# A second split buffer for projected q and k columns, and a planner that keeps TensorE on products of one width

## The chip, the cores and the metric

One NeuronCore of a Trainium2 chip runs the whole program. The metric is the device time of one execution in microseconds, as the median of the runs shown. TensorE (PE) multiplies, VectorE (DVE), ScalarE (ACT) and GpSimd (POOL) do the elementwise work, and SyncE (SP) issues nearly all DMAs.

## The reference, cut to what matters

One step of a two-layer decoder trunk in float32, for a prompt of 2048 tokens of width 1024 and for 8 sample sequences of one new token each with 2048 cached ones. Every layer is one input projection, two mixers that run as parallel branches, one output projection and a LayerNorm.

```python
def even_mixer(x, past_kv, w_in, w_sp, b_sp):          # layer 0
    h = jnp.einsum('btd,de->bte', x, w_in)
    u, v, gate_a, q, k, vb, gate_b = _split(h, EVEN_SPLITS)   # 7 x 512 columns
    ...
    out_a = chunk_spatial_gate(u, v, w_sp, b_sp) * jax.nn.silu(gate_a)
    o = stick_breaking(q, k, v, q_pos, k_pos)          # 8 heads of 64
    out_b = o * jax.nn.silu(gate_b)

def stick_breaking(q, k, v, q_pos, k_pos):
    z = jnp.einsum('bqhd,bkhd->bhqk', q, k) * HEAD_DIM ** -0.5
    log_keep = jnp.where(mask, jax.nn.log_sigmoid(-z), 0.0)
    later = lax.cumsum(log_keep, axis=3, reverse=True) - log_keep
    att = jnp.where(mask, jnp.exp(jax.nn.log_sigmoid(z) + later), 0.0)
    return jnp.einsum('bhqk,bkhd->bqhd', att, v)
```

Layer 1 (`odd_mixer`) selects the 256 best keys of each query by an indexer (four small heads), does softmax attention over them with a relative bias (8 query heads, 2 key heads), and beside it pools causally over windows of 2 to 16 tokens.

## The kernel before, in words

The prompt is cut into four blocks of 512 tokens (i = 0 to 3). Layer 0 of a block is its first phase `p0(i)` (load x and transpose it, 28 projections of 128 columns each), then attention `mixer_b(i)`, then the output projection `out_proj`. Layer 1 is `p1a` and `p1b` (projections), `c_tiles` (index, selection and attention for each 128 queries) and another `out_proj`. The phases of different blocks run beside each other, so that TensorE gets projections while attention waits for other engines.

Products of float32 accuracy on the projections are made of three in float32r: a number is split into a high part, rounded to float32r, and the rest. `split` does it: ScalarE casts (line 637), VectorE or GpSimd subtracts (line 643). A projection (`proj`) is 8 x 3 products of 128x512 into a bank `pp` of PSUM (lines 724, 725, 726); the weights are loaded as `wr` and split into `wh` and `wl` (lines 648, 650, 653). Of the 28 projections of `p0` the first four are q and the next four are k. Each is split into a tile `q_hl` or `k_hl` of 128 x 2 x 512, and two DMAs store it to `qsc` or `ksc` in DRAM, from where attention loads it in another layout. All of these tiles share one tag, `hl`, with one buffer: the cast of the next must wait until both stores of the last have landed. For k a plain copy `kT` (line 872) is made as well, transposed on TensorE (`ps_k`, line 882) and written out.

In `mixer_b` a product `z` (line 1014) gives scores, ScalarE makes `P` of it (lines 1018, 1021), VectorE scans it (line 1028), TensorE transposes it (`ps_p`, line 1051) and multiplies by v (`av`, line 1060). In layer 1 the same steps are `z_c` (line 1756), `zt` with the maximum `mx` (line 1758) and the exponent (line 1774), the transposes `ps_pc` (line 1787) and `av_c` (line 1801). The index has `z_i` (line 1446). `av`, `av_c`, `ps_rb` (line 1821) and the sample group's `ps_sav` (line 1984) use half or a quarter of TensorE's columns, two or four such products side by side; the code calls their kind "h" and a group of them that write one bank is placed as one. All other products use the full array.

What sets the order on each engine is a planner, `Order`, that runs when the program is built. It knows all instructions, what each needs, and which buffers it takes; `cost` gives each a busy time and a latency in ns. `plan` places them in a list for each engine: among those that are ready, the one with the lowest rank, which is the latest start that `latest` allowed it in an earlier plan, in ns. `settle` makes 15 pairs of plans and keeps one; `keep` fixes that order as dependencies. So a changed cost or rule may move any instruction of the program, on each engine, but adds or removes none. A change from or to kind "h" is priced with `TILED`, 150 ns.

Of the kernel before, what the change touches and what calls it, by code (L numbers as in the profile page):

```python
# [22 lines left out]
P = 128  # L23
# [62 lines left out]
class Order:  # L86
# [1 line left out]

    ENGINES = {"PE": "PE", "DVE": "DVE", "Activation": "ACT", "Pool": "POOL", "SP": "SP"}
    SEM, DMA_START, DMA_END, RATE = 200, 700, 1500, 280.0  # L90
    TILED = 150
    GUESSES = ((1.0, 200), (1.0, 250), (1.04, 230))
    ROUNDS, DRAWS, SPREAD = 5, 2, 0.05
    TAIL = {"ACT": 100, "POOL": 45, "DVE": 75}
# [136 lines left out]
    def cost(self, n):  # L231

        i, e = self.ins[n], "PE" if self.halves(n) else self.eng[n]
        aps = self.aps(i)
        if e is None or not aps:
            return (400, 400) if type(i).__name__ == "BassTileConditionalBlock" else (30 if e else 0, 30)
        if i.opcode == "TensorLoad":
            return 1300, 1300
        k = max(self.size(x) for x in aps)
        ps = any(self.space(x) == PSUM for x in aps)  # L240
        full = [x for x in i.ins if getattr(x, "bass_ap", None) is not None and self.size(x) > 1]
        if "DMA" in i.opcode:
            out = [x for x in i.outs if getattr(x, "bass_ap", None) is not None][0]
            size = math.prod(n for _, n in out.ap) * (2 if out.dtype == BF16 else 4)
            runs = []
            for x in aps:
                r = 1
                for s, n in reversed(list(x.ap)):
                    if s != r:
                        break  # L250
                    r *= n
                runs.append(r)
            return 65 if e == "SP" else 900, size / (self.RATE * (1.2 if min(runs) >= 512 else 0.93))
        if e == "PE":
            k = self.size(i.outs[0])
            if i.is_transpose:
                return 109, 270
            if i.ins[0].dtype == F32R:
                return max(59, 3 + 0.4455 * k), 0.444 * k + 170
            if self.halves(n):  # L260
                return max(109, 1.8 * k * tuple(i.tile_size)[1] / P), max(222, 1.7 * k) + 170
            return max(223, 6 + 1.67 * k), max(222, 1.75 * k) + 170
        name = re.sub(r"_\d+$", "", i.outs[0].bass_ap.tensor.name)
        c = BUSY.get(f"{e} {name} {i.opcode} {k}")
        if c is not None:
            return c, c + self.TAIL[e]
        if e == "ACT":
            c = 70 + (0.82 if ps else 0.87) * k if i.opcode == "TensorCopy" else 70 + 0.83 * k if ps else 200 + 0.93 * k
            return c, c + 100
        if e == "POOL":  # L270
            c = {"TensorTensor": 15 + 2.4 * k, "Iota": 50 + 0.9 * k, "Memset": 40}.get(i.opcode, 180 + 0.78 * k)
            return c, c + 45
        ptr = sum(getattr(x, "bass_ap", None) is not None and self.size(x) == 1 for x in i.ins) if k > 1 else 0
        if getattr(i, "is_tensor_tensor_scan", False):
            c = 40 + 2.23 * k
        elif i.opcode == "TensorScalarPtr" and not ps and len(full) == 1 and len(i.outs) == 1:
            c = 65 + 0.54 * k + 60 * ptr
        elif i.opcode == "TensorScalarPtr" and len(i.outs) > 1:
            c = 150 + 1.05 * k
        else:  # L280
            c = 65 + 1.04 * k + 60 * ptr
        return c, c + 75
# [157 lines left out]
    def plan(self, rank):  # L440
# [41 lines left out]
        while count < N:  # L482
            while back and back[0][0] <= now:
                _, g, x = pop(back)
                free[g] += 1
                gone[g].append(x)
                take(g, now)
            while due and due[0][0] <= now:
                n = pop(due)[1]
                if eng[n] is not None:  # L490
                    push(ready[eng[n]], (rank[n], n))
                    continue
                count += 1
                for m in succ[n]:
                    release(m, now)
            moved, late = False, []
            for e, q in ready.items():
                while q and idle[e] <= now:
                    n, until = q[0][1], hold.get(self.OTHER.get(e), 0.0)
                    if ports[n] and until > now:  # L500
                        free_ = [x for x in q if not ports[x[1]] and now + cost[x[1]][0] <= until + self.SLACK]
                        if not free_:
                            late.append(until)
                            break
                        n = min(free_)
                        q.remove(n)
                        heapq.heapify(q)
                        n = n[1]
                    else:
                        pop(q)  # L510
                    s, (busy, lat) = now, cost[n]
                    if ports[n]:
                        hold[e] = s + max(40, busy - self.RELEASE[e])
                    if e == "PE" and now > idle[e] + 1 and kinds[n] == kind:
                        busy, lat = busy + self.RESTART, lat + self.RESTART
                    if e == "PE" and kinds[n] != kind:
                        s += self.TILED if "h" in (kinds[n], kind) else 0
                        kind = kinds[n]
                    self.begun[n] = s
                    if self.dma[n]:  # L520
                        dma_end = max(s + self.DMA_START, dma_end) + lat
                        done[n] = dma_end + self.DMA_END
                    else:
                        done[n] = s + lat
                    idle[e] = s + busy
                    self.order[e] += [*self.before.get(n, ()), *self.group.get(n, (n,))]
                    count += 1
                    moved = True
                    for m in succ[n]:
                        release(m, s + 1 if e == "PE" and eng[m] == "PE" else done[n] + self.SEM)  # L530
                    for t in tiles[n]:
                        g, u = home[t], self.uses[t]
                        if n == u[0]:
                            open_[g] = True
                            for m in u[1:]:
                                release(m, s)
                            take(g, s)
                        users[t] -= 1
                        if not users[t]:
                            push(back, (max(done[m] for m in u) + self.SEM, g, t))  # L540
            if not moved:
                then = [q[0][0] for q in (due, back) if q] + [idle[e] for e in ready if ready[e]]
                then = [x for x in then if x > now] + late
                assert then or count == N
                now = max([now] + [min(then)] if then else [now])
# [68 lines left out]
class Body:  # L614
# [230 lines left out]
    def p0(self, i, smp=None):  # L845
# [14 lines left out]

        for m in range(4):
            ps = yield from pj(12 + m)
            hl = self.loc.tile([P, 2, TB], F32R, tag="hl", name="q_hl", bufs=self.bufs["hl"])
            self.split(hl[:, 0], hl[:, 1], ps, "act", "dve")
            for a in range(2):
                nc.sync.dma_start(self.qsc[i][2 * m + a].rearrange("c p n -> p c n"),
                                  hl[64 * a:64 * a + 64].bitcast(F32))

        for m in range(4):
            ps = yield from pj(16 + m)  # L870
            kT = self.tok("kT")
            nc.scalar.copy(kT, ps)
            hl = self.loc.tile([P, 2, TB], F32R, tag="hl", name="k_hl", bufs=self.bufs["hl"])
            self.split(hl[:, 0], hl[:, 1], ps, "act", "dve")
            for a in range(2):
                nc.sync.dma_start(self.ksc[i][2 * m + a].rearrange("(c p) n -> p c n", c=2),
                                  hl[64 * a:64 * a + 64].bitcast(F32))

            def k_tail(m=m, kT=kT):
                pt = self.ps("ps_k", [P, NT, P])  # L880
                for t in range(NT):
                    nc.tensor.transpose(pt[:, t, :], kT[:, t * P:(t + 1) * P], self.idf)
                kt = self.tmp("k_tok").rearrange("p (t c) -> p t c", t=NT)
                nc.scalar.copy(kt, pt)
                nc.sync.dma_start(kv[rows, 0, m * P:(m + 1) * P].rearrange("(t p) c -> p t c", p=P), kt)

            tails.append(k_tail)
# [1583 lines left out]
```

## Time and profile before

| | |
|---|---|
| median of 3 runs | 2861.96 us (2861.57 to 2862.91) |
| the profiled execution's own time | 2859.05 us |
| its span, first to last instruction | 2857.3 us |
| mean granted TensorE clock | 0.975 |
| busy: PE, DVE, ACT, POOL | 95%, 72%, 56%, 27% |
| DMA | 523.50 MB, mean 183 GB/s |

Rows of a timeline read: start in us, duration in us, engine, line, operation, what it writes and reads, shapes, how many in a row were merged, and in brackets how long the engine had been idle and what ended that. A duration of a product on PE runs into the next one's, since products overlap: the time that a product holds the engine is read from start to start. Rows of waits read: engine and line, what it waited for, us in total, times, longest.

### The profile page before, as it was taken

To read this page: it belongs to the slowest core of one execution; us is meant where nothing else is said; L and a number is where in the kernel's file an instruction comes from. 1 tells how busy PE (TensorE), PEld (TensorE's weight loads), DVE (VectorE), ACT (ScalarE), POOL (GpSimd) and SP (SyncE) were. 2 spreads that over 40 slices of the span, in tenths; PEclk is the share of its full clock that TensorE was granted. 3 is DMA by queue.
4 is the path that set the end of the run, shared out by engine and by line. 5 is a ranking of instruction groups with operands and counts; after the bars stand their busy time and mean duration, and the time that the engine had idled before them with its cause. 6 is when DMAs were issued, how large, how long until landed. Compare 5 with 4: busy or idle time off the path is not lost. (4 is left out here: it accounts for less than half of the span.)

```text
span 2857.3 us, 52362 instructions
## 1 busy us (share of the span) xinstructions
PE 2708.1 (95%) x17490; PEld 2160.9 (76%) x17490; DVE 2058.0 (72%) x5557; ACT 1608.3 (56%) x3216; POOL 764.7 (27%) x1040
## 2 busy tenths in 40 slices
PE   7999999999999999998899999999989999999996
PEld 6886777867777687777567777777857889798985
DVE  3375467685766776646877888897898677888865
ACT  2433333344443435434566777786686677788863
POOL 0001103120110412123332432334321353435222
PEclk9999999999999999998999999999989999999998
DMA  7565867597677659545575456433656566667462
GB/s 216 165 181 172 257 198 227 175 292 212 186 211 206 217 176 299 164 148 157 148 198 160 142 166 165 125 100 100 192 181 162 173 210 182 209 202 254 134 196 70
DMA packets 536591, 523.50 MB, mean 183 GB/s; under 512 B 43183, under 2 KB 408904, under 8 KB 536287
## 3 DMA queue, kind: packets, MB, share of 16 engines
q1 hardware_dynamic: 526439, 484.29, 56.5%
q0 software_dynamic: 9856, 35.66, 3.9%
q8 instruction: 139, 2.28, 0.3%
q14 instruction: 157, 1.29, 0.1%
HBM read 430.27 MB, written 89.73 MB: 182 GB/s over the span
## 5 line engine op out<-in xcount | busy, mean ns | idle before, releaser
L724 PE MATMUL pp<-xh,wh 128*128 128x512 f32 (+1 forms) x1536 | 633.4, 416 | 10.9 <-ACT xh L637 3.8
L725 PE MATMUL pp<-xl,wh 128*128 128x512 f32 (+1 forms) x1536 | 616.9, 402 | 1.5 <-DVE xl L643 1.3
L726 PE MATMUL pp<-xh,wl 128*128 128x512 f32 (+1 forms) x1536 | 612.8, 400 | 0.0
L653 DVE TENSOR_TENSOR wl<-wr,wh 128x512 fp32r<-128x512 f32 x520 | 355.6, 703 | 203.5 <-ACT wh L650 192.1
L650 ACT CAST wh<-wr 128x1024 fp32r<-128x1024 f32 x260 | 270.1, 1039 | 344.9 <-PE pp L725 196.8
L724 PEld LDWEIGHTS pp<-xh,wh 128*128 128x128 f32 (+1 forms) x1536 | 288.1, 189 | 89.7 <-issue 22.7
L725 PEld LDWEIGHTS pp<-xl,wh 128*128 128x128 f32 (+1 forms) x1536 | 289.6, 189 | 64.8 <-issue 11.4
L726 PEld LDWEIGHTS pp<-xh,wl 128*128 128x128 f32 (+1 forms) x1536 | 288.5, 188 | 61.5 <-issue 4.6
L1119 PE MATMUL pp_o<-wh,oh 128*128 128x256 f32 x1008 | 296.9, 297 | 9.0 <-DVE xres L1124 4.9
L1121 PE MATMUL pp_o<-wh,ol 128*128 128x256 f32 x1008 | 289.1, 291 | 4.9 <-POOL ol L643 4.7
L1120 PE MATMUL pp_o<-wl,oh 128*128 128x256 f32 x1008 | 290.6, 290 | 1.6 <-DVE wl L653 1.6
L1052 ACT COPY P<-ps_p 128x512 f32<-128x512 f32 (+1 forms) x320 | 166.5, 523 | 190.2 <-PE ps_p L1051 175.8
L1028 DVE TENSOR_TENSOR_SCAN P<-P,bfst 128x512 f32<-128x512 f32 x192 | 247.4, 1300 | 35.7 <-ACT P L1021 28.1
L1756 PE MATMUL z_c<-ksc,qc 128*128 128x512 f32 (+3 forms) x816 | 222.7, 355 | 17.9 <-DVE mx L1758 11.8
L1774 ACT ACTIVATE zt<-zt,nmax 128x512 f32<-128x512 f32 (+3 forms) x320 | 209.2, 656 | 47.7 <-DVE nmax L1762 46.0
L1789 ACT COPY zt<-ps_pc 128x512 f32<-128x512 f32 (+3 forms) x320 | 163.1, 521 | 99.2 <-PE ps_pc L1787 96.3
L1014 PE MATMUL z<-ks,q 128*128 128x512 f32 (+3 forms) x640 | 196.1, 393 | 16.1 <-DMA ks<-ksc 6.3
L1119 PEld LDWEIGHTS pp_o<-wh,oh 128*128 128x128 f32 x1008 | 194.5, 194 | 20.1 <-DVE xres L1124 6.1
L1121 PEld LDWEIGHTS pp_o<-wh,ol 128*128 128x128 f32 x1008 | 193.5, 193 | 11.0 <-POOL ol L643 7.4
L1120 PEld LDWEIGHTS pp_o<-wl,oh 128*128 128x128 f32 x1008 | 195.4, 194 | 6.1 <-DVE wl L653 2.7
L1743 POOL TENSOR_TENSOR nm<-nm,mk 128x256 f32<-128x256 f32 (+1 forms) x128 | 97.6, 764 | 380.3 <-DMA nm<-bft 180.8
L1758 DVE CUSTOM_DVE_ANT_0 zt<-z_c,mk 128x512 f32<-128x512 f32 (+3 forms) x256 | 149.3, 590 | 66.7 <-PE z_c L1756 49.0
(455 smaller groups left out, 5547.1 us busy)
## 6 DMA issues: line engine op xcount, KB each, us to landing
pg<-cache_b_kv SPq DMA_DIRECT2D x256, 256.0 KB
wr<-w_in_even SPq DMA_DIRECT2D x112, 512.0 KB
wr<-w_in_odd SPq DMA_DIRECT2D x76, 512.0 KB
wr<-w_out SPq DMA_DIRECT2D x68, 512.0 KB
ks<-ksc SPq DMA_DIRECT2D x80, 256.0 KB
ksc<-kcs SPq DMA_DIRECT2D x80, 256.0 KB
q<-qsc SPq DMA_DIRECT2D x64, 256.0 KB
qc<-qcs SPq DMA_DIRECT2D x128, 128.0 KB
```

The source lines that it names most:

```text
L650: nc.scalar.copy(hi, raw)
L653: e.tensor_tensor(lo[:, c], raw[:, c], hi[:, c].bitcast(F32), op=OP.subtract)
L724: nc.tensor.matmul(ps[:m], wh[:, kt, :m], xh[kt], start=a, stop=False)
L725: nc.tensor.matmul(ps[:m], wh[:, kt, :m], xl[kt], start=False, stop=False)
L726: nc.tensor.matmul(ps[:m], wl[:, kt, :m], xh[kt], start=False, stop=b)
L1014: nc.tensor.matmul(z[:, :n], q2[:, c, t * P:(t + 1) * P].bitcast(F32R), ks[:, :n].bitcast(F32R), start=c == 0, stop=c == 1)
L1028: nc.vector.tensor_tensor_scan(r, r, r, initial=ini, op0=OP.mult, op1=OP.bypass)
L1119: nc.tensor.matmul(ps[:, :256], oh[:, tt], wh[:, k], start=a, stop=False)
L1120: nc.tensor.matmul(ps[:, :256], oh[:, tt], wl[:, k], start=False, stop=False)
L1121: nc.tensor.matmul(ps[:, :256], ol[:, tt], wh[:, k], start=False, stop=b)
L1756: nc.tensor.matmul(z[:, :n], q2[:, c, jj % 2, :].bitcast(F32R), kk, start=c == 0, stop=c == 1)
L1774: nc.scalar.activation(zt, zt, AF.Exp, bias=nmx, accum_out=st["rs"][:, h, c:c + 1])
```

## The change

Three edits. The planner prices a float32r product of more than 16 rows of output at 110 ns at least (before: 59 ns for all); only products of 128 columns are touched by it, which `cost` gave 60 ns. When the instruction that TensorE would place next is of kind "h" and the last one placed was not, or the other way round, it takes instead the first ready one of the same sort as the last whose rank is at most `STAY` = 500 ns later, if there is one. And in `p0` the tiles of odd m, `q_hl` and `k_hl`, come from the pool `c0` instead of `loc`, each of which has one buffer for the tag: the projections take the two in turn.

```diff
-    TILED = 150
+    TILED, STAY = 150, 500
...
-                return max(59, 3 + 0.4455 * k), 0.444 * k + 170
+                return max(60 if i.outs[0].ap[0][1] <= 16 else 110, 3 + 0.4455 * k), 0.444 * k + 170
...
                     n, until = q[0][1], hold.get(self.OTHER.get(e), 0.0)
+                    if e == "PE" and (kinds[n] == "h") != (kind == "h"):
+                        same = [x for x in q if (kinds[x[1]] == "h") == (kind == "h") and x[0] <= q[0][0] + self.STAY]
+                        if same:
+                            n = min(same)[1]
+                            q.remove(min(same))
+                            heapq.heapify(q)
+                            push(q, (-math.inf, n))
...
-            hl = self.loc.tile([P, 2, TB], F32R, tag="hl", name="q_hl", bufs=self.bufs["hl"])
+            hl = (self.c0 if m % 2 else self.loc).tile([P, 2, TB], F32R, tag="hl", name="q_hl", bufs=self.bufs["hl"])
...
-            hl = self.loc.tile([P, 2, TB], F32R, tag="hl", name="k_hl", bufs=self.bufs["hl"])
+            hl = (self.c0 if m % 2 else self.loc).tile([P, 2, TB], F32R, tag="hl", name="k_hl", bufs=self.bufs["hl"])
```

The lines of the changed kernel after the planner's new rule have numbers that are higher by 7: line 637 of before is 644 there, line 1801 is 1808.

What the plan makes of it, at two places. First ScalarE in the q projections of block 1, from the second `q_hl` to the fourth and the weights behind it. `L1021` is `P` of attention on block 0, `s_pr` and `s_sgm` are the sample group's. Before:

```order
L637 CAST q_hl<-pp 128x512
L650 CAST wh<-wr 128x1024
L1021 ACTIVATE P<-z 128x128
L1021 ACTIVATE P<-z 128x256
L1955 ACTIVATE s_pr<-ps_sz 128x128
L1956 ACTIVATE s_sgm<-ps_sz 128x128
L637 CAST q_hl<-pp 128x512
L650 CAST wh<-wr 128x1024
L1021 ACTIVATE P<-z 128x384
L1021 ACTIVATE P<-z 128x512
L637 CAST q_hl<-pp 128x512
L650 CAST wh<-wr 128x1024
```

and in the changed kernel, from the first `q_hl` of that block:

```order
L644 CAST q_hl<-pp 128x512 x2
L657 CAST wh<-wr 128x1024
L1028 ACTIVATE P<-z 128x128
L1028 ACTIVATE P<-z 128x256
L657 CAST wh<-wr 128x1024
L644 CAST q_hl<-pp 128x512
L1962 ACTIVATE s_pr<-ps_sz 128x128
L657 CAST wh<-wr 128x1024
L1963 ACTIVATE s_sgm<-ps_sz 128x128
L644 CAST q_hl<-pp 128x512
L657 CAST wh<-wr 128x1024
L879 COPY kT<-pp 128x512
```

The casts stand closer together, with fewer exponents of attention between them: from the first cast of q to the last of k there were 39 rows on ScalarE in block 1 (each buffer told apart) and there are 29 now.

Second TensorE in layer 1's attention beside the sample group's index (`ps_sk`, `ps_sl`). Before:

```order
L1787 MATMUL ps_pc<-idf,zt 128x128 x4
L1756 MATMUL z_c<-ksc,qc 128x128 x2
L1756 MATMUL z_c<-ksc,qc 128x512
L2134 MATMUL ps_sl<-s_qb,s_tmp 128x16 x4
L1801 MATMUL av_c<-zt,vsc 64x128 x8
L1787 MATMUL ps_pc<-idf,zt 128x128
L1756 MATMUL z_c<-ksc,qc 128x512
L1801 MATMUL av_c<-zt,vsc 64x128 x8
```

and in the changed kernel:

```order
L1794 MATMUL ps_pc<-idf,zt 128x128 x4
L1763 MATMUL z_c<-ksc,qc 128x128
L1763 MATMUL z_c<-ksc,qc 128x512 x2
L2134 MATMUL ps_sk<-idf,s_kp 128x128 x4
L1808 MATMUL av_c<-zt,vsc 64x128 x16
L2141 MATMUL ps_sl<-s_qb,s_tmp 128x16 x4
```

Two groups of 8 half-width products became one run of 16; the second score product of `z_c` that stood between them went ahead of both. In the whole order there were 281 runs of kind "h" on TensorE and there are 255 now, of 1673 such products among 15336.

## The prediction

> **What bounds the kernel now.** I read the page first, then the stages, then the waits of TensorE and ScalarE, then single places in the timeline. The page's first part says that TensorE is the bound: 95% of the span, and VectorE, the next, 72%.
>
> ```profile
> span 2857.3 us, 52362 instructions
> PE 2708.1 (95%) x17490; PEld 2160.9 (76%) x17490; DVE 2058.0 (72%) x5557; ACT 1608.3 (56%) x3216; POOL 764.7 (27%) x1040
> ```
>
> So the time is TensorE's work plus its bubbles (span less busy: 2857.3 - 2708.1 = 149 us) plus what is lost to a lower clock. The stages show where: columns are the stretch, its length, busy time of PE, PEld, DVE, ACT and POOL, then PEclk, DMA share and GB/s.
>
> ```profile
> core 0: us, PE busy (x) PEld busy (x) DVE busy (x) ACT busy (x) POOL busy (x), PEclk, DMA share, GB/s
> 274.00:340.00 66.00, 61.10 (x294) 46.16 (x293) 30.07 (x71) 25.28 (x46) 10.35 (x25) 0.97 0.83 244
> ...
> 570.00:650.00 80.00, 75.73 (x371) 54.91 (x370) 65.41 (x100) 38.29 (x70) 18.85 (x31) 1.00 0.92 293
> ...
> 1060.00:1137.00 77.00, 77.00 (x400) 55.77 (x399) 52.23 (x83) 42.73 (x74) 19.17 (x26) 1.00 0.86 278
> ...
> 1280.00:1440.00 160.00, 131.05 (x810) 102.48 (x808) 122.99 (x326) 80.35 (x183) 62.71 (x98) 0.88 0.57 161
> ...
> 2000.00:2110.00 110.00, 93.94 (x700) 76.90 (x700) 94.97 (x390) 78.33 (x186) 37.86 (x45) 0.92 0.68 204
> ```
>
> The first three are the q and k projections of token blocks 1, 2 and 3: 4.9 and 4.3 us of bubbles, and none in block 3. The last two are the passage from layer 0's pools to the mixed ones and the start of the last part: 29.0 and 16.1 us, with the clock down to 0.88 and 0.92.
>
> A bubble costs more than its length. At 297.75 TensorE had waited 2.24 us, and after it a product took 0.43 us from start to start (299.20 to 299.62, 300.05) where it takes 0.23 otherwise:
>
> ```profile
> 296.38 0.59 ACT L637 CAST q_hl<-pp 128x512 fp32r<-128x512 f32 x1 [3.41 <-DMA qsc<-q_hl]
> ...
> 297.00 0.69 DVE L643 TENSOR_TENSOR q_hl<-pp,q_hl 128x512 fp32r<-128x512 f32 x1 [3.15 <-ACT q_hl L637]
> ...
> 297.75 0.80 PE L724 MATMUL pp<-xh,wh 128*128 128x512 f32 x1 [2.24 <-DVE q_hl L643]
> ...
> 298.19 1.25 SPq L866 DMA_DIRECT2D qsc<-q_hl  x2
> ...
> 299.20 0.63 PE L724 MATMUL pp<-xh,wh 128*128 128x512 f32 x1
> ...
> 299.62 0.63 PE L725 MATMUL pp<-xl,wh 128*128 128x512 f32 x1
> ...
> 300.05 0.63 PE L726 MATMUL pp<-xh,wl 128*128 128x512 f32 x1
> ...
> 304.57 0.59 ACT L637 CAST q_hl<-pp 128x512 fp32r<-128x512 f32 x1 [5.77 <-DMA qsc<-q_hl]
> ...
> 305.93 0.50 PE L724 MATMUL pp<-xh,wh 128*128 128x512 f32 x1 [0.94 <-DVE q_hl L643]
> ```
>
> ```profile
> 297.60:301.00 3.40, 3.25 (x8) 2.58 (x9) 3.00 (x6) 1.19 (x3) 1.38 (x4) 0.50 0.88 222
> 301.00:304.40 3.40, 3.40 (x17) 2.80 (x16) 0.72 (x1) 0.00 (x0) 2.25 (x9) 1.00 0.85 251
> ```
>
> In these two equal stretches 8 and 17 products were made: half the work, so 1.7 us lost behind a bubble of 2.24. The Trainium skill ("TensorE: Matmul & The Clock Gate", section "What's actually happening") says that the array falls to half rate after an idle window of about 3.4 us; here 2.24 us sufficed, so the trace disagrees. By the page this clock loss would not exist, and the first term below would be 1.7 us smaller.
>
> **The change, part by part.** (1) The second buffer. The rows above show what one buffer costs: the store of q_hl is issued at 298.19 and the next cast may start at 304.57, 6.4 us later, while a projection is 24 products of 0.23, 5.5 us. ScalarE waits in its queue, and the copies queued behind that cast wait with it:
>
> ```profile
> ACT q_hl L637 <- DMA qsc<-q_hl: 32.1, 10, 5.8
> ...
> ACT k_hl L637 <- DMA qsc<-q_hl: 7.5, 3, 3.6
> ...
> ACT k_hl L637 <- DMA ksc<-k_hl: 6.3, 5, 3.1
> ```
>
> That is 45.9 us of ScalarE, which has them to spare. What reaches TensorE is less. In block 1 the two bubbles above, 2.24 + 0.94. In block 2 three: transposes that need kT, whose copy stood behind a cast that had waited 5.50; scores that need the bank freed by an exponent behind a cast that had waited 1.14; and a projection that needs its bank back:
>
> ```profile
> 600.81 0.59 ACT L637 CAST q_hl<-pp 128x512 fp32r<-128x512 f32 x1 [5.50 <-DMA qsc<-q_hl]
> 601.29 0.59 ACT L872 COPY kT<-pp 128x512 f32<-128x512 f32 x1
> ...
> 601.93 0.66 PE L882 MATMUL ps_k<-idf,kT 128*128 128x128 f32 x4 [0.68 <-ACT kT L872]
> ```
>
> ```profile
> 612.17 0.59 ACT L637 CAST k_hl<-pp 128x512 fp32r<-128x512 f32 x1 [1.14 <-DMA qsc<-q_hl]
> 612.66 0.39 ACT L1021 ACTIVATE P<-z 128x256 f32<-128x256 f32 x1
> ```
>
> ```profile
> 613.10 0.73 PE L1014 MATMUL z<-ks,q 128*128 128x512 f32 x2 [1.35 <-ACT P L1021]
> ...
> 632.49 0.50 PE L724 MATMUL pp<-xh,wh 128*128 128x512 f32 x1 [0.39 <-DVE k_hl L643]
> ```
>
> Sum 3.18 + 2.42 = 5.6, with the clock 7.3. Two buffers allow a reuse after two projections, 11 us, against 0.59 + 0.69 + 0.5 + 6.4, about 8.2 us from cast to free buffer: the wait should go. The upper end of the gain is 7.3. The lower end is nothing, by block 3, where the same buffer cost TensorE no time (77.00 of 77). I take 5.5, nearer to the rows of the places themselves, less a part for the next wait in line: a projection that comes sooner asks sooner for its weights. The cast and the subtraction, the stores (64 in the four blocks) and their bytes stay as they are. SyncE's queue gets the stores closer together: in block 2 the DMA share is 0.92 already, so that a weight load can come later there; I cost that at nothing because each weight is loaded a projection ahead, and if that cover goes, bubbles of the same size as now come back. In block 0 TensorE has other work at each of the waits, so nothing.
>
> (2) Staying with half-width products. Each change between the two kinds of product costs time on TensorE, the bound, with no cover:
>
> ```profile
> 2198.54 0.39 PE L726 MATMUL pp<-xh,wl 128*128 128x512 f32 x1
> 2198.77 0.39 PE L1446 MATMUL z_i<-kid,qi 128*128 128x512 f32 x1
> 2199.09 0.66 PE L1801 MATMUL av_c<-zt,vsc 128*64 128x128 f32 x8
> 2199.68 0.51 PE L1446 MATMUL z_i<-kid,qi 128*128 128x512 f32 x1
> ```
>
> ```profile
> 2193.23 1.09 PE L1801 MATMUL av_c<-zt,vsc 128*64 128x128 f32 x16
> 2194.26 0.44 PE L1787 MATMUL ps_pc<-idf,zt 128*128 128x128 f32 x2
> ```
>
> Going in: 2198.77 to 2199.09 is 0.32 against 0.23, so 0.09. Going out: 8 products hold TensorE for 0.59 us and 16 for 1.03, so 8 more cost 0.44 and 0.15 is the end's. A run that is joined to another saves between 0.18 (0.09 both ways) and 0.24; I take 0.20. In the order of before stand 281 runs of such products, in that of the changed kernel 255, of the same 1673 products. So 26 x 0.20 = 5.2 us, with ends of 4.7 and 6.2. The Trainium skill ("TensorEngine Tiling (Array Packing)", section "Key Properties") says that a change of tiling mode drains the array; with a whole overlap lost (0.39 - 0.23 = 0.16 each way) that would be 8.3 us, but the row shows 0.09 on the way in.
>
> (3) The plan's price of a product of 128 columns goes from 60 to 110 ns, of which there are 256 (z, z_i, z_c on the diagonal). The products stay as long as they are; only their places in the order move. 256 x 0.05 = 12.8 us of TensorE time that the plan did not know of, most of it in the parts with index and softmax. Bounds: all of it could have become bubbles (gain of 12.8), or the new places make as much new waiting (loss of 12.8). I take 0, as no wait in the profile can be tied to it.
>
> (4) All that was not touched is placed anew too, since one plan orders the whole program. Outside of (1), the start and the tail there are some 100 us of bubbles, made of waits of a few us; I take their sum as unchanged.
>
> Sum: 5.5 + 5.2 = 10.7 us. The profiled execution took 2859.05 us, so 2848.4; the median of the runs is 2.9 higher, 2861.96, and the same difference gives 2851.3. I say 2851.
>
> **The rivals.** A: the price in (3) frees the tight stages. 1280 to 1440 and 2000 to 2110 hold 29.0 + 16.1 = 45 us of bubbles; a third of it back is 15 us more: 2836. For it: these are the stages with the products it prices. Against it: their largest waits are for loads and for VectorE.
>
> B: the gain is eaten. The new places bring bubbles of about 10 us, of the 100 that are dealt anew, and the time stays within 0.2% (5.7 us, about what a measurement of this kernel can tell from no change): about 2861. For it: block 3 shows that the buffer can be hidden; and on a bound of 95% a planned wait is easily swapped for another. This holds also the case that the second buffer does nothing and (2) alone is left: 2862 - 5.2 = 2857.
>
> C: slower. Longer runs of half-width products, and full-width ones that are preferred for up to half a us, put off the next head's scores z_c; VectorE's maximum on them, the exponent and the transposes come later, and TensorE runs dry in the last part. The waits of this sort now, and what one costs:
>
> ```profile
> PE z_c L1756 <- DVE mx L1758: 11.8, 9, 3.5
> ```
>
> ```profile
> 2629.39 0.80 PE L1756 MATMUL z_c<-ksc,qc 128*128 128x512 f32 x1 [2.28 <-DVE mx L1758]
> ```
>
> ```profile
> 2629.20:2632.40 3.20, 3.01 (x13) 2.97 (x14) 3.13 (x23) 0.96 (x3) 0.00 (x0) 0.51 1.11 297
> ```
>
> 2.28 us and half of 3.2 us at clock 0.51 make 3.9. Three more eat the 10.7 us, five more make it slower by over 5.7 (19.5 less 10.7); with six it is 2851 + 23 = 2874. Against it: a product may be put off by no more than half a us of its due time, and the runs get only a tenth fewer.
>
> **How the numbers follow.** The forecast 0.42, its own range 2845 to 2856 (the upper ends of (1) and (2) give 13.5 us of gain, 2848.5, the lower 4.7 us, 2857, and a few us of (4) on the better side); A 0.20; B 0.22; C 0.16. Faster by over 0.2%: forecast and A, 0.62; within: B, 0.22; slower: C, 0.16. The range reaches from 2834, which holds nearly the whole of A, to 2868, the lower half of C: some 0.17 are left out.
>
> **What would show it.** In the changed profile: the waits of q_hl and k_hl on the stores of qsc and ksc fall from 45.9 us to under 10; TensorE's bubbles in the q and k projections of blocks 1 and 2 fall from 9.2 to under 5, with no stretch of clock 0.5 there; runs of x16 of av_c where there were two of x8; VectorE's and ScalarE's busy times the same within 1%. The prediction is wrong if the bubbles outside those projections sum to more than now by over 6 us, with more stretches at 0.5, or if the z_c waits on mx are above 20 us.

## The result, and the profile after

The changed kernel took 2839.24 us (median of 7 runs, 2834.56 to 2844.05) against 2861.96 of before (7 runs, 2850.69 to 2864.59): a ratio of 0.9926, 95% interval 0.9912 to 0.994. That is 22.7 us less, where 10.7 were forecast. The profiled execution took 2836.16 us.

The page of the changed kernel:

```profile
span 2834.5 us, 52431 instructions
PE 2697.2 (95%) x17490; PEld 2165.2 (76%) x17490; DVE 2063.6 (73%) x5557; ACT 1603.6 (57%) x3216; POOL 773.4 (27%) x1040
```

TensorE's busy time fell by 10.9 us (2708.1 before) and its bubbles by 11.9 (149.2 to 137.3). VectorE and ScalarE work as long as before, within 0.3%. The three stretches of the q and k projections of blocks 1, 2 and 3, and then the two tight passages behind layer 0, in the columns of the prediction (all of it 4 to 25 us earlier than before):

```profile
270.00:335.00 65.00, 63.44 (x314) 48.34 (x314) 29.61 (x74) 25.52 (x45) 7.42 (x20) 1.00 0.78 235
560.00:640.00 80.00, 80.00 (x407) 63.46 (x407) 60.46 (x100) 34.56 (x61) 10.02 (x14) 1.00 0.99 313
1045.00:1120.00 75.00, 75.00 (x386) 54.94 (x384) 43.80 (x63) 37.94 (x65) 18.02 (x18) 1.00 0.84 264
```

```profile
1255.00:1415.00 160.00, 133.42 (x825) 104.87 (x824) 123.36 (x330) 81.76 (x186) 66.25 (x100) 0.87 0.56 161
1975.00:2085.00 110.00, 97.71 (x708) 80.81 (x707) 90.61 (x365) 72.35 (x177) 37.88 (x45) 0.92 0.71 208
```

The projections of blocks 1 and 2 have 1.56 us of bubbles where there were 9.2, at full clock, and block 2 does 407 products in the 80 us in which it did 371. Of ScalarE's 45.9 us of waits on the stores only this is left in the whole span:

```profile
ACT q_hl L644 <- DMA qsc<-q_hl: 0.3, 1, 0.3
```

The weight loads are less well ahead than before. In block 2 the DMA engines are busy for 0.99 of the stretch, and ScalarE's waits for these loads over the whole span (first before, then after) rose from 9.2 to 26.6 us. No wait of TensorE on weights stands in these stretches.

```profile
ACT wh L650 <- DMA wr<-w_in_even: 9.2, 6, 2.4
```

```profile
ACT wh L657 <- DMA wr<-w_in_even: 26.6, 12, 5.8
```

Where in the program did the 22.7 us come from? I cut each trace at two places that every version has: the first transpose `ps_bf` of the bias (near 256 us) and layer 1's first index product `z_i` (1263 to 1304 us in the versions below). Between them lies nearly all of layer 0's prompt work with its projections in blocks 1 to 3; behind the second cut all the rest. Before:

```profile
255.87:1290.80 1034.93, 1005.53 (x5375) 766.08 (x5376) 684.42 (x1185) 431.80 (x783) 192.28 (x283) 0.99 0.69 213
1290.80:2857.20 1566.40, 1465.51 (x10682) 1202.95 (x10681) 1248.84 (x4073) 1083.90 (x2252) 548.72 (x706) 0.97 0.55 165
```

and after:

```profile
257.25:1264.74 1007.49, 993.73 (x5388) 764.55 (x5388) 689.09 (x1185) 428.45 (x782) 187.06 (x285) 0.99 0.71 217
1264.74:2834.40 1569.66, 1466.56 (x10670) 1208.06 (x10669) 1248.29 (x4073) 1082.96 (x2253) 563.53 (x708) 0.96 0.56 165
```

All of the gain, and more, lies in layer 0: 27.4 us less there, 3.3 more behind it. The 27.4 are 15.6 of bubbles (29.4 to 13.8) and 11.8 of busy time. Of the busy time 6.8 are clock: the time at which the granted clock was half sums to 27.2 us in this stretch before and to 13.7 after, and half of the difference is lost work. Runs of half-width products in the stretch went from 73 to 64, 1.8 us at 0.20; some 3 us stay unexplained. Behind the second cut it goes the other way: 2.2 us more of bubbles, and 115.8 us at half clock where there were 105.6.

Of the 15.6 us of bubbles in layer 0 only some 5.6, the prediction's sum, stood behind waits on the stores. Others went at places that no edit aims at. In this stretch the first two rows here, of before, are waits at the sample group's `ps_sz` and at an output projection; after, the first is gone and the second is 0.4 us. A new wait came (third row, after):

```profile
PE ps_sz L1951 <- DVE s_z L1945: 4.7, 2, 3.4
...
PE pp_o L1119 <- DVE gu L834: 3.1, 1, 3.1
```

```profile
PE ps_a L931 <- DVE gv L841: 7.3, 2, 3.7
```

### The profile page after: what moved, and what is told of

It is laid out like the page before. It is cut to its first block, busy times and chain, and to the rows that moved or that the text cites. A ratio compares the mean times of both kernels' runs of the same rounds, so it can differ in the third digit from the quotient of the medians.

```text
span 2834.5 us, 52431 instructions
## 1 busy us (share of the span) xinstructions
PE 2697.2 (95%) x17490; PEld 2165.2 (76%) x17490; DVE 2063.6 (73%) x5557; ACT 1603.6 (57%) x3216; POOL 773.4 (27%) x1040
## 5 line engine op out<-in xcount | busy, mean ns | idle before, releaser
L731 PE MATMUL pp<-xh,wh 128*128 128x512 f32 x1536 | 626.0, 411 | 4.8 <-ACT xh L644 3.7
L731 PEld LDWEIGHTS pp<-xh,wh 128*128 128x128 f32 x1536 | 288.3, 189 | 72.3 <-issue 8.2
L1059 ACT COPY P<-ps_p 128x512 f32<-128x512 f32 (+2 forms) x320 | 166.0, 522 | 189.0 <-PE ps_p L1058 181.0
L1763 PE MATMUL z_c<-ksc,qc 128*128 128x512 f32 (+3 forms) x816 | 221.4, 356 | 23.0 <-DVE mx L1765 19.5
L1021 PE MATMUL z<-ks,q 128*128 128x512 f32 (+3 forms) x640 | 196.8, 392 | 11.7 <-DMA ks<-ksc 4.6
L1509 ACT ACTIVATE mk<-ix,tk_tn 128x384 int8<-128x384 f32 (+13 forms) x140 | 183.5, 1311 | 35.7 <-DVE tk_tn L1559 20.9
```

What stands on the lines that cost most here:

```text
L731: nc.tensor.matmul(ps[:m], wh[:, kt, :m], xh[kt], start=a, stop=False)
L1021: nc.tensor.matmul(z[:, :n], q2[:, c, t * P:(t + 1) * P].bitcast(F32R), ks[:, :n].bitcast(F32R), start=c == 0, stop=c == 1)
L1763: nc.tensor.matmul(z[:, :n], q2[:, c, jj % 2, :].bitcast(F32R), kk, start=c == 0, stop=c == 1)
```

## The experiments

The theories. 1: the waits on the one buffer were themselves the loss, and lifting them is the gain. 2: two buffers let the planner place the projections closer, and the new places are the gain. 3: fewer changes of width. 4: chance; the planner's result hangs on details, and this one fell well. Two more came up later. 5: the edits together make the gain whatever the chance. 6: two buffers shorten the stretch of layer 0 by 15 to 40 us on any deal, while the parts behind it are a lottery. By a deal I mean one outcome of the planner among those that meaningless changes of its numbers give.

**Order and buffers apart.** Two kernels part what the change ties together. `two_old` has two buffers, but its planner is told of one, so that every engine has the order of before. `one_new` has one buffer, but its planner is told of two: the order of the changed kernel with the old limit.

```diff
 two_old: before, with the tiles of odd m from c0, and in Order
+        own = next(t.tag for t in tc.info.tiles if t.name.startswith("qi_hl"))
+        self.tag = lambda t: own if t.startswith(("q_hl", "k_hl")) else self.tiles[t].tag
 one_new: the changed kernel, with all these tiles from loc, and in Order
+        self.tag = lambda t: c0 if t in odd else self.tiles[t].tag
```

> The order of before on every engine, word for word, with two buffers for q_hl and k_hl: only the waits on the stores change. Theory 1 (the lifted waits themselves are the gain of layer 0): 10 to 18 us under before, 2844 to 2852, and the bubbles at the q and k projections of blocks 1 and 2 gone. Theory 2 (the gain is in the new placing that two buffers allow): at most the 5.6 us of bubbles and 1.7 of clock that stand directly behind such waits, 2855 to 2860. Theory 3 (fewer changes of width): 2862.

> The order of the changed kernel on every engine, with one buffer for all q_hl and k_hl as before: the casts now stand closer together than one buffer allows. Theory 1 and 2: the gain is lost and more, 2860 to 2885, with ScalarE's waits for the stores of q_hl and k_hl above 60 us. Theory 3: little of the gain is lost, 2840 to 2848.

Against the kernel before, `two_old` measured 0.9988 (0.9974 to 1.0002) and `one_new` 1.0012 (0.9997 to 1.0027). Neither half alone gives anything that can be told from no change. For `two_old` that fits theories 2 and 3, but not theory 1, which expected 10 to 18 us. For `one_new` theories 1 and 2 expected the whole gain to be lost, as it was, with more than 60 us of waits on the stores (they came to 58.9); theory 3 expected most of it to stay. The stretches say what each half does. `two_old`, layer 0 and then the projections of blocks 1 and 2:

```profile
256.80:1285.38 1028.58, 1006.09 (x5376) 765.92 (x5376) 684.99 (x1185) 430.26 (x783) 193.14 (x283) 0.99 0.69 214
```

```profile
274.00:340.00 66.00, 63.96 (x324) 47.89 (x323) 32.98 (x78) 27.23 (x49) 11.39 (x26) 1.00 0.87 270
570.00:650.00 80.00, 77.07 (x376) 56.80 (x375) 64.76 (x102) 34.92 (x66) 17.50 (x29) 1.00 0.96 301
```

and `one_new`, layer 0:

```profile
258.27:1281.35 1023.08, 995.80 (x5387) 765.78 (x5388) 688.69 (x1185) 429.50 (x782) 188.02 (x285) 0.99 0.70 214
```

With the old order the lifted waits shorten layer 0 by 6.3 us: the bubbles of blocks 1 and 2 fall from 9.2 to 5.0, those of the whole stretch from 29.4 to 22.5, and of the waits on stores of `qsc` and `ksc` 0.8 us is left. With the new order the second buffer is worth 15.6 us there (1023.08 to 1007.49). What happens when the new order meets one buffer stands in the waits of `one_new`, over the whole span, and at one place in block 2:

```profile
ACT q_hl L647 <- DMA qsc<-q_hl: 36.1, 9, 8.5
...
ACT k_hl L647 <- DMA ksc<-k_hl: 16.4, 8, 5.1
...
ACT k_hl L647 <- DMA qsc<-q_hl: 6.4, 3, 3.5
```

```profile
558.15 0.59 ACT L647 CAST q_hl<-pp 128x512 fp32r<-128x512 f32 x1
...
561.29 1.32 SPq L877 DMA_DIRECT2D qsc<-q_hl  x2
...
566.23 0.58 ACT L647 CAST q_hl<-pp 128x512 fp32r<-128x512 f32 x1 [6.15 <-DMA qsc<-q_hl]
566.71 0.38 ACT L1064 COPY P<-ps_p 128x256 f32<-128x256 f32 x1
...
567.14 0.90 PE L1063 MATMUL ps_p<-idf,P 128*128 128x128 f32 x3 [5.68 <-ACT P L1064]
```

The same two casts in the changed kernel:

```profile
557.60 0.59 ACT L644 CAST q_hl<-pp 128x512 fp32r<-128x512 f32 x1
...
559.39 0.61 ACT L644 CAST q_hl<-pp 128x512 fp32r<-128x512 f32 x1
559.96 0.37 ACT L1059 COPY P<-ps_p 128x256 f32<-128x256 f32 x1
```

Two buffers let the plan put two casts 1.8 us apart. With one they are 8.1 apart, the copy of attention's `P` queued behind the second waits with it, and TensorE stands for 5.68 us at transposes that need the bank. The old order kept the casts apart, with the exponents and copies of attention between them, so that its waits cost little; but it also held the projections to that pace. From the first cast of q to the last of k it took 55.5 us in block 1 and 70.6 in block 2; two buffers in the old order make that 50.5 and 69.4, and the changed kernel takes 40.0 and 48.0 (read from the starts of the casts). So on this deal theory 1 explains about 6 us of layer 0's 27, and the rest needs the new order. How much of that order comes from the buffer and how much from the planner's two edits, this pair can't say.

**Each edit re-planned.** `hl` is the second buffer alone, `stay_floor` the two edits of the planner without it, `hl_stay` the buffer with the rule `STAY`, `hl_floor` the buffer with the price of 110 ns.

```diff
 hl:         before + hl = (self.c0 if m % 2 else self.loc).tile(...)
 stay_floor: before + the rule STAY + max(60 if ... <= 16 else 110, ...)
 hl_stay:    the changed kernel, with the price as before: max(59, 3 + 0.4455 * k)
 hl_floor:   the changed kernel, without the rule STAY
```

> The second buffer alone, planned anew; 282 runs of half-width products as against 281 before. Theory 1 and 2: 2862 less 15 to 18 us, 2844 to 2847, all of it ahead of 1290 us. Theory 3: 2862. Theory 4 (a new plan deals all bubbles anew, whatever the edit): anywhere between 2850 and 2874, with changes in all parts.

> The two edits of the planner without the second buffer; 252 runs of half-width products as against 281. Theory 3 with the measured 0.19 us a run: 29 x 0.19 = 5.5 us, 2856, spread over the parts with attention. Theory 1 and 2 say the same 2856 or 2862 and no gain ahead of 1290 us beyond 2 us. Theory 4: 2850 to 2874.

> The second buffer and the rule to stay, without the price of 110 ns; 255 runs of half-width products. Sum of the two alone: 0.9991 and at most 0.9992, so 0.998. Theory 5 with the price being idle: 0.993. Theory 4: 0.993 to 1.003.

> The second buffer and the price of 110 ns, without the rule to stay; 284 runs. Sum of the two alone: 0.999. Theory 5 with the rule being idle but for its 29 runs x 0.19 = 5.5 us: 0.995. Theory 4: 0.993 to 1.003.

| | ratio to before (95%) | runs of kind "h" | layer 0's stretch, us | behind it, us |
|---|---|---|---|---|
| before | | 281 | 1034.9 | 1566.4 |
| hl | 0.9991 (0.9976 to 1.0006) | 282 | 1021.0 | 1575.6 |
| stay_floor | 0.9992 (0.9979 to 1.0004) | 252 | 1027.1 | 1568.0 |
| hl_stay | 0.9972 (0.996 to 0.9983) | 255 | 1009.4 | 1592.1 |
| hl_floor | 0.9957 (0.9942 to 0.9973) | 284 | 1018.3 | 1581.0 |
| changed kernel | 0.9926 (0.9912 to 0.994) | 255 | 1007.5 | 1569.7 |

The stretches are from single profiled executions, and the last two columns do not hold what lies ahead of the first cut. Differences of a few us between them can't be read: the profiled executions lie up to 9.3 us off the median of their kernel, and the kernel before itself took 2855.30, 2863.45 and 2861.23 us in the three rounds of experiments. The ratios are taken within a round.

`hl` shortens layer 0 by 14 us and loses 9 of them behind it, where it changed nothing on purpose. In layer 0 both sides of the change count: 14.0 for the buffer, 7.9 for the planner's two edits, 27.4 for all, which is 5.5 more than the sum. Taken at face value, some 6 of the 27 us are theory 1, about 8 more are theory 2 (the buffer, planned anew), and the other 13 came only with the planner's edits. That split is argued, not shown, as each of these kernels is another outcome of the planner. The buffer alone gives most of the closer placing: 42.5 and 48.9 us from the first cast of q to the last of k in blocks 1 and 2, where `stay_floor` has 44.3 and 76.1. Of the planner's two edits it seems to be the rule `STAY` that counts here: the price of 110 ns does nothing to be seen (1009.4 without it, 1007.5 with it). Fewer changes of width, theory 3, are not enough for that, as 9 runs fewer in this stretch are worth 1.8 us; which new places make the rest, no run takes apart.

The expectations for whole times fared badly: theories 1 and 2 had 15 to 18 us for `hl`, theory 3 had 5.5 for `stay_floor`, and neither can be told from no change. So the next question was how large chance is.

**The same change on other deals.** The planner's first plans start from three guesses of how long an engine takes to hear of another, in ns. Moving them by 3 or 6 ns has no meaning; it deals the order anew. I did so on both sides of the change.

```diff
-    GUESSES = ((1.0, 200), (1.0, 250), (1.04, 230))
+    GUESSES = ((1.0, 203), (1.0, 253), (1.04, 233))    # before_redeal, after_redeal
+    GUESSES = ((1.0, 197), (1.0, 247), (1.04, 227))    # before_deal_c, after_deal_c
+    GUESSES = ((1.0, 206), (1.0, 256), (1.04, 236))    # before_deal_d, after_deal_d
```

> The kernel before with the same edit without meaning. Theory 4: the ratio to before may be anything from 0.993 to 1.007. Theory 5: 0.998 to 1.002, as the one-sided edits gave.

> The changed kernel with the planner's three guesses of a wait between engines moved by 3 ns (200, 250, 230 to 203, 253, 233): an edit without meaning that deals the order anew. Theory 4 (the gain is a lucky deal): the ratio to before is as likely at 0.997 to 1.003 as at 0.993. Theory 5 (the edits together make the gain, whatever the deal): 0.990 to 0.995.

> The kernel before, with the planner's guesses at 197, 247 and 227 ns: a third deal. Theory 6 (two buffers shorten layer 0's stretch by 15 to 40 us on any deal, and the parts behind it are a lottery in which both kernels drew well): layer 0's stretch of 1023 to 1049 us with 30 to 37 us of bubbles in it, the parts behind it together 1566 to 1610; ratio to before 1.000 to 1.012. Theory 4 (all is lottery): layer 0's stretch anywhere from 1007 to 1049.

> The changed kernel with the same guesses. Theory 6: layer 0's stretch of 1007 to 1015 us with 14 to 18 us of bubbles in it; the parts behind it 1566 to 1610; ratio to the same deal of before 0.985 to 0.997. Theory 4: stretch anywhere from 1007 to 1049, and a ratio to the same deal of before on either side of 1.

> The kernel before, with the guesses at 206, 256 and 236 ns: a fourth deal. Theory 6 and 4 as for the third.

> The changed kernel with the guesses of the fourth deal. Theory 6 and 4 as for the third. Under theory 4 one of these two deals beats the changed kernel in one case of two; under theory 6 in fewer, since its parts behind layer 0 took 1570 us, near the best of all so far.

Columns 2 and 3 are ratios to the kernel before as it was. The fourth is the quotient, with the two half-widths added in squares (too wide rather than too narrow, since both were timed against the same runs).

| guesses | without the change | with it | with over without |
|---|---|---|---|
| as they were | 1 | 0.9926 (0.9912 to 0.994) | 0.9926 (0.9912 to 0.994) |
| +3 ns | 1.0105 (1.0087 to 1.0124) | 1.0011 (0.9997 to 1.0024) | 0.9907 (0.988 to 0.993) |
| -3 ns | 1.0074 (1.0048 to 1.01) | 1.0017 (0.9999 to 1.0035) | 0.9943 (0.991 to 0.998) |
| +6 ns | 1.0078 (1.0048 to 1.0108) | 0.9994 (0.9976 to 1.0012) | 0.9917 (0.988 to 0.995) |

Layer 0's stretch in these six, the three without the change first:

```profile
254.90:1304.15 1049.25, 1012.08 (x5384) 769.72 (x5385) 689.03 (x1188) 431.00 (x783) 184.44 (x289) 0.98 0.69 210
```

```profile
255.57:1295.91 1040.34, 1008.59 (x5386) 767.04 (x5386) 692.59 (x1188) 430.40 (x782) 191.27 (x288) 0.99 0.70 212
```

```profile
256.83:1297.12 1040.29, 1007.87 (x5389) 766.40 (x5389) 686.55 (x1186) 431.95 (x783) 181.35 (x285) 0.99 0.70 211
```

```profile
256.96:1266.33 1009.37, 994.83 (x5387) 766.25 (x5388) 688.53 (x1186) 429.90 (x782) 195.22 (x286) 0.99 0.71 217
```

```profile
257.40:1269.50 1012.10, 990.65 (x5389) 763.10 (x5390) 688.46 (x1186) 430.72 (x782) 190.80 (x282) 0.99 0.71 217
```

```profile
257.04:1263.41 1006.37, 991.09 (x5387) 762.31 (x5388) 692.30 (x1186) 430.33 (x782) 190.06 (x286) 1.00 0.72 218
```

Three things follow. The gain belongs to the edits: on four deals out of four the change takes 0.6 to 0.9%, on average 0.9923 (0.990 to 0.995, from the spread of the four), and theory 4 falls.

That reading was not the one forecast for the pair at +3 ns: its ratios to the kernel before as it was, 1.0011 and 1.0105, are not what theory 5 expected (theory 4 allowed the first and not the second), and the quotient was taken afterwards. For the two later pairs theory 6 had the quotient at 0.985 to 0.997 beforehand, and both came inside.

Layer 0's stretch is 1035 to 1049 us without the change and 1006 to 1012 with it, 32 less on average, with no overlap; 16 of the 32 are bubbles, 9 are clock. The q and k projections are packed on every deal: 53 to 56 us in block 1 and 70 to 73 in block 2 without the change, 40 and 48 to 56 with it. So theory 6 holds in that half for the three edits together, and theory 5 as far as the whole time goes; the deals always switched all three edits, so they do not tell the buffers' share. One forecast was missed: 21.5 us of bubbles in the stretch with the change at -3 ns, where 14 to 18 were expected.

And chance is as large as the change: 3 or 6 ns without meaning moved either kernel by 0.7 to 1.05%, and the versions with the original guesses are each the fastest of their four. So the ratios of single edits above, each on a deal of its own, cannot be read to better than about 1%; the quotient on equal deals can.

The other half of theory 6 stays open. Behind layer 0 the four deals without the change took 1566, 1581, 1584 and 1579 us, the four with it 1570, 1609, 1595 and 1592. That is 14 us longer on average with the change, and it is all clock: the time at half clock there is 106, 113, 124 and 135 us without the change and 116, 169, 156 and 154 with it, and half of the difference is 14. In both rows the deal with the original guesses lies well off its fellows, and four do not tell a cost from chance. A third of the 14 may lie in which executions were profiled: at +3 ns the one with the change took 9.3 us more than its kernel's median and the one without 5.2 less. `hl`, `hl_stay` and `hl_floor` are longer there too (1576, 1592, 1581) and those with the old buffer or the old order on the original guesses are not (1567 for `two_old`, 1569 for `one_new`, 1568 for `stay_floor`); but the other three deals without the change, with old buffer and old order, are as long. A faster layer 0 might well meet its loads, or the sample group's work, in a worse place later; no run here tests that.

## Why the prediction was right or wrong

The time, 2839, lies in the range and in "faster", but the gain is twice that forecast, and one wrong step kept the larger part of what happened in layer 0 out of the sum. That the change shows against the kernel before as it was is in part luck: on the other three deals the changed kernel takes as long as that one (0.9994 to 1.0017).

By the two profiled spans 22.8 us were gained: 7.6 are bubbles in the q and k projections of blocks 1 and 2, 4.3 bubbles elsewhere, 1.7 clock, 5.2 width if the price of 0.20 holds, and 4 are in no term. The forecast had 5.5 for the first, clock and bubbles together, 5.2 for the width, and nothing for the rest.

- **Term (1), the buffer.** As an estimate of what the waits cost in the old order it was about right: 5.5 us taken, 7.3 at most, and `two_old` measured 6.3 in layer 0 from one execution of each (its whole time, 0.9988, can't be told from no change). Its signs came too: waits on the stores from 45.9 us to 0.3, bubbles of blocks 1 and 2 from 9.2 to 1.56 and full clock. The weight loads, whose delay was costed at nothing, are less well ahead: ScalarE waits 17.4 us more for them, and nothing of that reached TensorE in layer 0.
- **Term (4), the step that failed.** It took the bubbles outside the places of (1) as unchanged, since chance would deal them anew. In layer 0 they were not dealt by chance. There the bubbles outside those places fell from 20.2 to 12.2 us, the time at half clock fell by 13.5, and on four deals the stretch got shorter by 27 to 40 us. One buffer had forced the plan to spread the projections, and with two it packs them (70.6 us to 48.0 in block 2); the planner's edits add to the gain. Of the 27 us on this deal 6 are waits lifted in the old places, and the other 21 came with the new order. How the closer placing of the projections makes the bubbles elsewhere in layer 0 go is not shown. Over the whole program the sum that (4) kept fixed fell by 4.3 only, as the bubbles ahead of and behind layer 0's stretch grew by 3.8. The sign stood in the orders shown ahead of the prediction: 39 rows on ScalarE from the first to the last cast of block 1, then 29. I read them as a change of order and gave that no price. A bound was to be had: layer 0's stretch before has 29.4 us of bubbles and 27.2 us at half clock, which is worth half: 43 us that a better order may take from.
- **Term (2), the width.** Its count is as the orders say, 26 runs fewer. Its price, 0.20 a run, could not be told from chance on whole times. Taking bubbles and half of the time at half clock from the span, the seven kernels with the rule keep 2625 us on average and the seven without it 2635. They have 29 runs fewer, 5.8 us at 0.20, so the rule may be worth nearly twice its price; which products make the other 4 or 5 us is open.
- **Term (3), the price of 110 ns,** taken as 0: `hl_stay`, which lacks it, has the same stretch of layer 0 within 2 us. Its whole time is 0.9972 against 0.9926 with it, but that difference lies behind layer 0, where deals differ by as much. Neither confirmed nor refuted.
- **Rival A** gave nearly the right time for the wrong reason. The two tight passages hold 26.6 and 12.3 us of bubbles where they held 29.0 and 16.1, and the parts behind layer 0 took 3.3 us longer all the same.
- **Rival B** is what `hl` looks like (0.9991): a gain in layer 0, given back elsewhere. It did not come out for the whole change on any deal, when the change is compared with the kernel before on the same guesses.
- **Rival C** was there to see and did not decide:

```profile
PE z_c L1763 <- DVE mx L1765: 19.5, 13, 4.7
```

That is 7.7 us more than before, half a us under the line that I had drawn. Whether the rule causes it stays open: the same edits on the deals at +3, -3 and +6 ns have 19.5, 11.3 and 9.5 us of this wait, and the seven kernels with the rule have 15.8 on average, the seven without it 11.3. It may be part of what is lost behind layer 0.

## What to carry to other kernels

Where an order is planned around a buffer, the waits in the trace show only what the plan could not hide; what it paid to hide the rest stands in the pace of the work. So lift the limit and plan anew before judging it, and run the crossed pair (new buffers in the old order, old buffers in the new order) to see which half pays. And where one plan orders the whole program, measure how far a meaningless change moves the time before reading the ratio of a meaningful one, compare on several equal deals, and look at the stretch that the change aims at.

## What the runs showed of the hardware

The same program with the same instructions, in orders that differ by 3 or 6 ns in a guess, took 2862 to 2892 us; with the change, 2839 to 2868. What the orders differ in is above all waiting and clock: of the 28.1 us between the profiled spans of the kernel before on the original guesses and at +3 ns, 14.2 are bubbles and 10.7 are half of the difference in time at half clock (143.0 to 164.5 us).

Behind the wait of 5.68 us in `one_new` TensorE again worked at half clock, for all of the first stretch here and about half of the second:

```profile
567.10:570.50 3.40, 3.36 (x10) 2.77 (x11) 2.87 (x5) 2.09 (x4) 0.00 (x0) 0.50 1.05 257
570.50:573.90 3.40, 3.40 (x13) 2.72 (x12) 2.99 (x4) 0.00 (x0) 0.86 (x1) 0.76 0.86 267
```

The granted clock of 0.50 and 0.76 over 3.4 us each makes 2.5 us that this wait cost beyond its length; the wait of 2.24 us in the prediction cost 1.7. The time at half clock does not simply follow the bubbles. In layer 0 the changed kernel has half of both (29.4 us of bubbles to 13.8, 27.2 us at half clock to 13.7). Behind layer 0, on the average of the four deals, it has 2 us more of bubbles and 29 us more at half clock.
